# Another order of the input units and small copies by ScalarE instead of GpSimd, in a hybrid SSD, S5 and attention layer

## The chip, the core and the metric

The kernel runs on one core of a Trainium2 chip. The metric is the device time of one launch in microseconds (us). Each run of a kernel is timed several times and the median is given. A profile is one further execution, with its own time. The engines are PE (TensorE, matmuls), DVE (VectorE), ACT (ScalarE), POOL (GpSimd) and SP (SyncE, which issues nearly all DMAs here).

## The reference, cut to what matters

One layer of a streaming encoder on 528 prompt positions (16 of them learned) and 64 sample positions, 592 columns in all, D_MODEL = 1024. One input projection feeds three branches.

```python
h = rmsnorm(x, lp['norm_mix'])
y_a, conv_new, ssd_new = ssd_branch(h, z, xbc, dt, ...)      # conv of width 4, silu, chunked scan, gate silu(z)
y_b, s5_re, s5_im = s5_branch(h @ w_u, ...)                  # complex diagonal scan
o_c = stick_breaking(q, [k_hist, k], [v_hist, v])            # attention with q/k norm
mix = gates[0]*(y_a @ w_lift_a) + gates[1]*glu(gelu(y_b)) + gates[2]*(o_c @ w_lift_c)
x = x + mix @ w_out
x = x + square(relu(rmsnorm(x) @ w_up)) @ w_down

def causal_dwconv(x, hist, w, b):
    xp = concatenate([hist, x], axis=1)
    y = b + sum(xp[:, k:k + T] * w[k] for k in range(4))
    return y, xp[:, -3:]                                     # the last three columns are an output
# s5_branch:  x_t = a * x_{t-1} + B u_t (complex);  y = Re(C x) + d * u;  outputs also x at the last position
```

The convolution's last three input columns and the S5's last states, for prompt and sample, are outputs. All of it is float32.

## The kernel before, in words

**Units.** Every product with a weight is cut into units of 128 output columns (`units()`, L71). A unit's weights, 128 x 1024, are loaded by SP into one of three `w_raw` buffers (L287). ACT copies them rounded into `w_hi` (L253), DVE subtracts to get `w_lo` (L217, the line of the helper `tt`). PE then makes, for each half of the 592 columns, 24 matmuls: w_hi with the high and the low part of the activations (L336, L337), w_lo with the high part (L338). They go to one of three PSUM buffers (`ps_d`), which ACT, mostly, evacuates.

**The order of the units.** `ORDER` (L59) is a string that `mixed()` reads: x is a unit of the SSD's convolution input (`do_xbc`, ten), z one of its gate (`do_z`, eight), a, b, c the sums' gates. `units()` puts four u units (the S5's input) and twelve q, v, k units ahead of them, and the later products behind.

**An x unit.** `do_xbc` takes a tile `pre` (three buffers, tag "ea", shared with the q, k and v units), zeroes its first three columns (L559), copies three columns of the old state into it (L560), evacuates PSUM into it (L564 to L567), copies its edges into the output tile `conv_o` (L569, L570), and forms the convolution (`cv`: L572 on ACT, then L574 three times on DVE), its sigmoid and product (`cs`), which SP stores to `x_scr` (L578). `conv_out` (L1210) is stored once, when all ten are there.

**Beside the units.** The S5, the attention and the SSD are Python generators that are advanced a step at a time between units, by credits (`PACE`), so their instructions lie among the units' in each engine's order. The S5 (`s5()`) first has eight steps q, then a scan on DVE (L803), from which come `x_r` and `x_i` (DVE, tags d_r and d_i). Four copies, 128x16 each, put the last states into `so` (L816), which SP stores to `s5_out` (L817; the profile calls it s_out). `xs` is filled from x_r and x_i, half by ACT (L826) and half by DMA (L828). Eight iterations follow: in each, eight DMAs fill a tile `tz` (L834, two buffers, so that iteration 2's waits for PE's last use in iteration 0), and PE multiplies tz with `ub` (L847) and `oc` with `xs` (L849), in turns, into `ps_y`. ACT and DVE make y from it (`gsq`, L855 and L856; `y_sb`).

**Who sets the order.** A scheduler of the framework lists each engine's instructions once, ahead of time. Each engine then runs its own list strictly in order, waiting on semaphores where its inputs or buffers aren't ready. SP's list is one queue too: a DMA whose data isn't ready holds back all DMAs behind it.

Of the kernel before, what the change touches and what calls it, by code (L numbers as in the profile page):

```python
# [11 lines left out]
AF = mybir.ActivationFunctionType  # L12
# [4 lines left out]
TP, TS = 528, 64  # L17
# [8 lines left out]
XW = 3 + TP + 3 + TS  # L26
# [29 lines left out]
NC_ = _fields(CST, [("ident", 128), ("tri", 128), ("blk", 128), ("msk", 128), ("msk_s", 64), ("eye2", 16)])  # L56


ORDER = "x" * 10 + "z" * 8 + "a" * 8 + "b" * 8 + "c" * 8  # L59


def mixed():
    n = dict.fromkeys("xzabc", 0)
    out = []
    for c in ORDER:
        out.append(({"x": "xbc", "z": "z", "a": "g1", "b": "g2", "c": "g0"}[c], n[c]))
# [110 lines left out]
def body(tc, io):  # L177
    nc = tc.nc
    V, S, G, PE, SP = nc.vector, nc.scalar, nc.gpsimd, nc.tensor, nc.sync
# [4 lines left out]
    with ExitStack() as ctx:  # L184
# [13 lines left out]
        A = lambda n, i=0, w=1: pa[:, PA[n][0] + i:PA[n][0] + i + w]  # L198
# [17 lines left out]
        def tt(e, o, a, b, op):  # L216
            e.tensor_tensor(o, a, b, op=op)  # L217
# [31 lines left out]
        def sigmoid(a, out, scale=1.0):  # L249
            S.activation(out, a, AF.Sigmoid, scale=scale)  # L250
# [128 lines left out]
        def dense(u, xh, xl, evac, kt=8, base=0, w=None, parts=live, weave=False):  # L379
            if w is None:  # L380
                w, i = fetch(u)
                ahead(i)
            if weave:
                pss = [psd.tile([128, 512], F32, name="ps_d", tag="d") for _ in parts]
                for k in range(kt):
                    for ps, cols in zip(pss, parts):
                        mm3(ps[:, :cols.stop - cols.start], w[0], w[1], 1, xh[:, k:k + 1], xl[:, k:k + 1], cols,
                            base=base + k, start=k == 0, stop=k == kt - 1)
                for ps, cols in zip(pss, parts):
                    evac(cols, ps[:, :cols.stop - cols.start])  # L390
                return w
            for cols in parts:
                n = cols.stop - cols.start
                ps = psd.tile([128, 512], F32, name="ps_d", tag="d")
                mm3(ps[:, :n], w[0], w[1], kt, xh, xl, cols, base=base)
                with urgent():
                    evac(cols, ps[:, :n])
                side(kt)
            return w
# [32 lines left out]
        for k in range(8):  # L432
            x, g = xt[:, k, :], gm[:, k:k + 1]
# [59 lines left out]
        conv_o = keep.tile([128, 10, 6], F32, name="conv_o", tag="conv_o")  # L493
# [10 lines left out]
        def etile(n, tag, w=T, dt=F32):  # L504
            return ev.tile([128, 608], dt, name=n, tag=tag, bufs=BUFS[tag])[:, :w]
# [51 lines left out]
        def do_xbc(m):  # L557
            pre = etile("pre", "ea", XW)
            G.memset(pre[:, 0:3], 0.0)  # L559
            G.tensor_copy(pre[:, 3 + TP:6 + TP], A("state_conv", 3 * m, 3))  # L560

            def evac(cols, ps):
                if cols.start == 0:
                    S.activation(pre[:, 3:3 + H], ps, AF.Copy)  # L564
                else:
                    S.activation(pre[:, 3 + H:3 + TP], ps[:, :TP - H], AF.Copy)
                    S.activation(pre[:, 6 + TP:], ps[:, TP - H:], AF.Copy)  # L567
            dense(("xbc", m), hh, hl, evac, parts=halves)
            G.tensor_copy(conv_o[:, m, 0:3], pre[:, TP:TP + 3])  # L569
            G.tensor_copy(conv_o[:, m, 3:6], pre[:, XW - 3:XW])  # L570
            c = etile("cv", "eb", CW)
            S.activation(c, pre[:, 0:CW], AF.Identity, scale=A("conv_w", 4 * m), bias=A("conv_b", m))  # L572
            for k in range(1, 4):
                V.scalar_tensor_tensor(c, pre[:, k:k + CW], A("conv_w", 4 * m + k), c, op0=OP.mult, op1=OP.add)  # L574
            s = etile("cs", "ec", CW)
            sigmoid(c, s)
            tt(V, s, s, c, OP.mult)
            SP.dma_start(x_scr[m], s)  # L578
# [141 lines left out]
        def s5():  # L720
# [30 lines left out]
            for q in range(8):  # L751
# [18 lines left out]
                z = psg.tile([128, 512], F32, name="ps_bs", tag="g")  # L770
# [11 lines left out]
                m = [sp.tile([128, 2, NX], F32, name="mo%d" % j, tag="mo%d" % j) for j in range(4)]  # L782
# [30 lines left out]
            tt(V, fl(x_i), fl(x_i), yy[:, 0, :], OP.add)  # L813
            so = new("so", [128, 4, 16])
            for j, (xx, c) in enumerate(((x_r, NB), (x_i, NB), (x_r, NX - 1), (x_i, NX - 1))):
                G.tensor_copy(so[:, j, :], xx[:, :, c])  # L816
            SP.dma_start(io["s5_out"], so)  # L817
            yield

# [9 lines left out]
            for it in range(8):  # L829
# [29 lines left out]
                if it % 2:  # L859
                    m = it // 2  # L860
# [562 lines left out]
        n1.release()  # L1423
        do_dt()
        pulls.append((s5(), PACE["s5"]))
        for m in range(4):
            do_qk("q", m, qg, q_scr, live)
# [3 lines left out]
        for n, m in mixed():  # L1431
            if n == "xbc":
                do_xbc(m)
                if m == 9:
                    pulls.append((ssd(), PACE["ssd"]))
            elif n == "z":
                do_z(m)
            else:
                do_gate(int(n[1]), m)
# [32 lines left out]
        for m2 in range(4):  # L1472
            w = None
            for j in range(2):
                m = 2 * m2 + j
# [25 lines left out]
        for m in range(8):  # L1501
            x = etile("xr", "eb")
# [159 lines left out]
```

## Time and profile before

| | |
|---|---|
| median of 3 runs | 1120.91 us (1119.19 to 1122.09) |
| the profiled execution | 1120.97 us, span 1119.2 us |
| mean granted clock | 0.994 |
| PE busy | 1100.5 us, 98% |
| DVE, ACT, POOL busy | 794.3, 539.6, 183.7 us |

The profile gives the busy time of each engine, windows (busy time, count of instructions and the granted TensorE clock of a stretch; 1.00 is 2.4 GHz), the chain of waits that ended last, and timelines. In a window's row the columns are the engines PE, PEld (weight load), DVE, ACT and POOL. A wait is written behind an arrow with the instruction that ended it. The S5's end (scan, states, eight iterations) lies between 193 and 281 us in this trace.

### The profile page before, as it was taken

Reading aid. Unit: us, or ns where it says so; the run is one execution under the profiler, and the core shown is the slowest. Engines: PE = TensorE matmul, PEld = TensorE weight load, DVE = VectorE, ACT = ScalarE, POOL = GpSimd, SP = SyncE. Lnnn points to the kernel's source line nnn. Section 1 sums busy time; section 2 is a strip of 40 time slices with the busy share of each in tenths; the row PEclk is TensorE's granted clock in tenths of the full one; section 3 lists DMA queues with packets and bytes.
Section 4 is the critical chain, followed back from the end, with each engine's and each line's share of the span. In section 5 each row is a group of like instructions: output and inputs, shape, how many; then the busy total and the mean of one; then the engine's idle time right before and its main releaser. Section 6 shows DMA issues by size and latency. Waiting matters only on the chain.

```text
span 1119.2 us, 21309 instructions
## 1 busy us (share of the span) xinstructions
PE 1100.5 (98%) x8532; PEld 1061.7 (95%) x8532; DVE 794.3 (71%) x1377; ACT 539.6 (48%) x896; POOL 183.7 (16%) x240
## 2 busy tenths in 40 slices
PE   9999999999999999999998999999999999999998
PEld 8998999999998999898788999999999999999998
DVE  7968579955667475549988754467866785786787
ACT  6455465523365455465668323355444444444443
POOL 2086256611000000005422300300000000000000
PEclk9999999989999999999999999999999999999999
DMA  7663224466754353277445543322232223223222
GB/s 275 147 145 115 84 90 125 110 165 165 241 177 138 113 179 133 89 255 257 129 146 167 151 134 99 99 75 94 76 102 88 75 77 115 74 76 129 79 81 80
DMA packets 80594, 144.04 MB, mean 129 GB/s; under 512 B 26512, under 2 KB 40688, under 8 KB 79984
## 3 DMA queue, kind: packets, MB, share of 16 engines
q1 hardware_dynamic: 80496, 142.69, 41.0%
q8 instruction: 67, 1.10, 0.4%
q14 instruction: 31, 0.25, 0.1%
HBM read 117.40 MB, written 24.38 MB: 127 GB/s over the span
## 4 chain that ended last, share of the span: by engine, by line
PE 80%; DVE 10%; POOL 3%; ACT 2%; DMA 2%; issue 2%; SPq 1%; DVEq 0%; ACTq 0%; POOLq 0%
PE ps_d L336 18%; PE ps_d L337 18%; PE ps_d L338 18%; PE ps_x L1581 3%; PE ps_x L1580 3%; PE ps_x L1582 3%; PE ps_o L895 2%; PE ps_z L895 2%; PE ps_y L1581 1%; PE ps_y L1580 1%; PE ps_y L1582 1%; DVE w_lo L217 1%; DVE ar L1272 1%; DVE ar L217 1%; POOL cm L217 1%
## 5 line engine op out<-in xcount | busy, mean ns | idle before, releaser
L336 PE MATMUL ps_d<-hh,w_hi 128*128 128x288 f32 (+1 forms) x864 | 260.5, 301 | 0.0
L338 PE MATMUL ps_d<-hh,w_lo 128*128 128x288 f32 (+1 forms) x864 | 260.0, 301 | 0.0
L337 PE MATMUL ps_d<-hl,w_hi 128*128 128x288 f32 (+1 forms) x864 | 260.0, 301 | 0.0
L253 ACT ACTIVATE w_hi<-w_raw 128x1024 fp32r<-128x1024 f32 (+1 forms) x150 | 151.8, 1012 | 220.7 <-PE ps_d L337 142.8
L217 DVE TENSOR_TENSOR w_lo<-w_raw,w_hi 128x1024 fp32r<-128x1024 f32 (+1 forms) x150 | 179.2, 1195 | 104.2 <-ACT w_hi L253 103.7
L337 PEld LDWEIGHTS ps_d<-hl,w_hi 128*128 128x128 f32 x864 | 164.5, 190 | 0.9 <-issue 0.3
L338 PEld LDWEIGHTS ps_d<-hh,w_lo 128*128 128x128 f32 x864 | 164.7, 191 | 0.5
L336 PEld LDWEIGHTS ps_d<-hh,w_hi 128*128 128x128 f32 x864 | 164.7, 191 | 0.4
L336 PE MATMUL ps_d<-x2h,w_hi 128*128 128x288 f32 x512 | 151.3, 296 | 0.0
L337 PE MATMUL ps_d<-x2l,w_hi 128*128 128x288 f32 x512 | 151.1, 295 | 0.0
L338 PE MATMUL ps_d<-x2h,w_lo 128*128 128x288 f32 x512 | 150.3, 295 | 0.0
L338 PEld LDWEIGHTS ps_d<-x2h,w_lo 128*128 128x128 f32 x512 | 96.2, 188 | 0.1
L336 PEld LDWEIGHTS ps_d<-x2h,w_hi 128*128 128x128 f32 x512 | 96.2, 188 | 0.1
L337 PEld LDWEIGHTS ps_d<-x2l,w_hi 128*128 128x128 f32 x512 | 96.2, 188 | 0.0
L253 ACT ACTIVATE w_hi<-ws 128x1024 fp32r<-128x1024 f32 x32 | 34.0, 1061 | 55.0 <-PE ps_y L1581 21.7
L1581 PE MATMUL ps_x<-ftl,w_hi 128*128 128x288 f32 x192 | 56.7, 295 | 0.5 <-DVE ftl L217 0.5
L1580 PE MATMUL ps_x<-fth,w_hi 128*128 128x288 f32 x192 | 56.8, 296 | 0.2 <-ACT s L1600 0.2
L1582 PE MATMUL ps_x<-fth,w_lo 128*128 128x288 f32 x192 | 56.4, 294 | 0.0
L1531 ACT ACTIVATE fr<-ps_d 128x288 f32<-128x288 f32 x64 | 25.7, 402 | 55.8 <-PE ps_d L338 55.8
L217 POOL TENSOR_TENSOR xe<-xd,tend 128x1024 f32<-128x1024 f32 (+2 forms) x6 | 11.6, 1942 | 234.4 <-DVE xd L217 210.1
L217 DVE TENSOR_TENSOR w_lo<-ws,w_hi 128x1024 fp32r<-128x1024 f32 x32 | 39.0, 1220 | 12.6 <-ACT w_hi L253 12.6
L906 DVE TENSOR_TENSOR_SCAN aw<-col,aw 128x400 f32<-128x400 f32 (+4 forms) x36 | 30.7, 899 | 17.3 <-ACT aw L250 17.2
(472 smaller groups left out, 2727.1 us busy)
## 6 DMA issues: line engine op xcount, KB each, us to landing
w_raw<-wts SPq DMA_DIRECT2D x150, 512.0 KB, 3.5
g_scr<-go SPq DMA_DIRECT2D x24, 288.0 KB, 2.8
gt<-g_scr SPq DMA_DIRECT2D x24, 288.0 KB, 3.1
ar<-ac_scr SPq DMA_DIRECT2D x4, 1024.0 KB, 7.2
x_scr<-cs SPq DMA_DIRECT2D x10, 297.5 KB, 2.9
xc<-x_scr SPq DMA_DIRECT2D x4, 640.0 KB, 7.0
xt<-xT SPq DMA_DIRECT2D x8, 296.0 KB, 5.7
z_scr<-zs SPq DMA_DIRECT2D x8, 288.0 KB, 4.6
```

The costliest lines, as they stand in the source:

```text
L217: e.tensor_tensor(o, a, b, op=op)
L253: S.activation(hi, x, AF.Copy)
L336: PE.matmul(ps, wh[:, c], xh[:, k, cols], start=start and k == 0, stop=False)
L337: PE.matmul(ps, wh[:, c], xl[:, k, cols], start=False, stop=False)
L338: PE.matmul(ps, wl[:, c], xh[:, k, cols], start=False, stop=stop and k == kt - 1)
L895: mm = lambda *a, **b: PE.matmul(*a, skip_group_check=True, **b)
L906: V.tensor_tensor_scan(x, one.to_broadcast([128, n]), x, 1.0, op0=OP.mult, op1=OP.mult)
L1272: V.tensor_scalar(ar[:n, h, :n], ar[:n, h, :n], acm[:n, c, h:h + 1], 0.0, op0=OP.subtract, op1=OP.min)
L1531: S.activation(r[:, cols], ps, AF.Relu)
L1580: PE.matmul(ps, w[0][:, o], fh[:, k], start=first and k == 0, stop=False, skip_group_check=True)
L1581: PE.matmul(ps, w[0][:, o], fl[:, k], start=False, stop=False, skip_group_check=True)
L1582: PE.matmul(ps, w[1][:, o], fh[:, k], start=False, stop=k == 3, skip_group_check=True)
```

## The change

The string of units begins with four z units, then the ten x units, then the other four z units. Three lines of `do_xbc` and one of `s5()` copy with ScalarE (`S.activation`, function Copy) what GpSimd copied: ten times three copies of 128x3, and four of 128x16.

```diff
-ORDER = "x" * 10 + "z" * 8 + "a" * 8 + "b" * 8 + "c" * 8
+ORDER = 'zzzzxxxxxxxxxxzzzzaaaaaaaabbbbbbbbcccccccc'
@@ do_xbc
-            G.tensor_copy(pre[:, 3 + TP:6 + TP], A("state_conv", 3 * m, 3))
+            S.activation(pre[:, 3 + TP:6 + TP], A("state_conv", 3 * m, 3), AF.Copy)
@@ do_xbc, behind dense(("xbc", m), ...)
-            G.tensor_copy(conv_o[:, m, 0:3], pre[:, TP:TP + 3])
-            G.tensor_copy(conv_o[:, m, 3:6], pre[:, XW - 3:XW])
+            S.activation(conv_o[:, m, 0:3], pre[:, TP:TP + 3], AF.Copy)
+            S.activation(conv_o[:, m, 3:6], pre[:, XW - 3:XW], AF.Copy)
@@ s5
-                G.tensor_copy(so[:, j, :], xx[:, :, c])
+                S.activation(so[:, j, :], xx[:, :, c], AF.Copy)
```

The numbers behind names are those of buffers; they differ between the two kernels. First SP's queue of the kernel before, from the second half of `xs` to the `tz` loads of the S5's third iteration (cs_2858 belongs to the eighth x unit):

```order
L828 DMA xs1_2385<-x_r_2323 64x1216
L828 DMA xs0_2384<-x_i_2324 64x1216
L817 DMA s5_out<-so_2331 128x64
L287 DMA w_raw_3164<-wts 128x1024
L578 DMA x_scr_223<-cs_2858 128x595
L1210 DMA conv_out<-conv_o_234 128x60
L834 DMA tz_2627<-kd_scr_225 16x4x128 x8
```

The same place in the kernel after (cs_2705 belongs to the second x unit):

```order
L828 DMA xs1_2362<-x_r_2311 64x1216
L828 DMA xs0_2361<-x_i_2312 64x1216
L817 DMA s5_out<-so_2319 128x64
L287 DMA w_raw_3021<-wts 128x1024
L578 DMA x_scr_223<-cs_2705 128x595
L834 DMA tz_2583<-kd_scr_225 16x4x128 x8
```

The x units stand later against the S5 there, so the store of `conv_out`, which needs all ten, has gone behind.

Next GpSimd's list of the kernel before, round the copies into `so`, with the edges of the last three x units (pre_2862, pre_2963, pre_3058):

```order
L569 COPY conv_o_234<-pre_2862 128x3
L570 COPY conv_o_234<-pre_2862 128x3
L816 COPY so_2331<-x_r_2323 128x16
L569 COPY conv_o_234<-pre_2963 128x3
L570 COPY conv_o_234<-pre_2963 128x3
L816 COPY so_2331<-x_i_2324 128x16
L816 COPY so_2331<-x_r_2323 128x16
L816 COPY so_2331<-x_i_2324 128x16
L559 MEMSET pre_3058 128x3
L560 COPY pre_3058<-pa_81 128x3
L569 COPY conv_o_234<-pre_3058 128x3
L570 COPY conv_o_234<-pre_3058 128x3
```

In the kernel after, ScalarE's list has these copies, here round `so`:

```order
L569 ACTIVATE conv_o_234<-pre_2818 128x3
L570 ACTIVATE conv_o_234<-pre_2818 128x3
L572 ACTIVATE cv_2910<-pre_2818,pa_81 128x595
L816 ACTIVATE so_2319<-x_r_2311 128x16
L826 ACTIVATE xs0_2361<-x_r_2311 64x1216
L816 ACTIVATE so_2319<-x_i_2312 128x16
L816 ACTIVATE so_2319<-x_r_2311 128x16
L816 ACTIVATE so_2319<-x_i_2312 128x16
L826 ACTIVATE xs1_2362<-x_i_2312 64x1216
L250 ACTIVATE cs_2705<-cv_2700 128x595
```

The copies stand between ScalarE's own work on x_r and x_i, behind the third x unit's L572. GpSimd keeps only the memsets L559 of this stretch.

Last, ScalarE's list of the kernel after where the state of the third x unit is copied into its `pre` (pre_2709), among the z units that now come first (`zs` is a z unit's evacuation, `rr` belongs to the S5's steps q):

```order
L253 ACTIVATE w_hi_2419<-w_raw_2221 128x1024
L250 ACTIVATE zs_2326<-ps_d_2381 128x288
L768 ACTIVATE rr_2108<-ps_r_2099 128x512
L560 ACTIVATE pre_2709<-pa_81 128x3
L250 ACTIVATE zs_2418<-ps_d_2425 128x288
L253 ACTIVATE w_hi_2511<-w_raw_2331 128x1024
L250 ACTIVATE zs_2418<-ps_d_2471 128x288
L564 ACTIVATE pre_2508<-ps_d_2517 128x296
```

The copy into pre_2709, which needs a buffer of tag "ea" to be free, stands ahead of evacuations of a z unit and of a weight's `w_hi`; in the kernel before it stood on GpSimd's list.

## Rows read from the trace of the kernel before

**Rows 1.** The page: busy time, share of the span and instructions of each engine.

```profile
PE 1100.5 (98%) x8532; PEld 1061.7 (95%) x8532; DVE 794.3 (71%) x1377; ACT 539.6 (48%) x896; POOL 183.7 (16%) x240
```

**Rows 2.** Windows of 40 us: length, PE, PEld, DVE, ACT, POOL, clock, DMA, GB/s.

```profile
200.00:240.00 40.00, 37.58 (x252) 37.38 (x251) 31.50 (x40) 17.60 (x30) 21.11 (x16) 0.87 0.55 150
...
840.00:880.00 40.00, 40.00 (x303) 40.00 (x302) 27.85 (x42) 17.52 (x32) 0.00 (x0) 1.00 0.25 82
```

**Rows 3.** The waits of PE: us in total, times, longest us.

```profile
PE ps_y L847 <- DMA tz<-kd_scr: 2.4, 1, 2.4
```

**Rows 4.** Timeline of PE: start us, us, what, idle before and its releaser.

```profile
218.07 0.39 PE L847 MATMUL ps_y<-ub,tz 128*128 128x73 f32 x2
...
228.44 0.67 PE L847 MATMUL ps_y<-ub,tz 128*128 128x73 f32 x2 [2.42 <-DMA tz<-kd_scr]
...
594.20 0.40 PE L336 MATMUL ps_d<-ybx,w_hi 128*128 128x288 f32 x1 [1.75 <-DVE mix L217]
```

**Rows 5.** Windows round the waits and the low clock.

```profile
228.40:238.90 10.50, 10.46 (x46) 10.49 (x47) 4.29 (x9) 1.98 (x5) 2.86 (x2) 0.51 0.71 198
238.90:249.40 10.50, 10.50 (x84) 10.50 (x83) 5.42 (x9) 3.89 (x7) 1.11 (x1) 1.00 0.43 89
282.00:287.00 5.00, 5.00 (x28) 4.95 (x28) 3.85 (x18) 1.80 (x3) 0.00 (x0) 0.66 0.82 248
...
596.00:606.00 10.00, 10.00 (x74) 9.83 (x74) 8.73 (x22) 7.69 (x12) 1.43 (x1) 1.00 0.75 258
```

**Rows 6.** Timeline of SP's DMA issues, 213 to 227 us.

```profile
213.11 0.46 SPq L828 DMA_DIRECT2D xs<-x_i  x1
220.62 0.35 SPq L817 DMA_DIRECT2D s_out<-so  x1
...
222.49 4.45 SPq L834 DMA_DIRECT2D tz<-kd_scr  x8
```

**Rows 7.** The chain that ended last, at the wait: start us, us, what.

```profile
226.51 1.80 DMA tz<-kd_scr
```

**Rows 8.** Timeline of POOL, 213 to 221 us.

```profile
213.07 1.96 POOL L816 COPY so<-x_r 128x16 f32<-128x16 f32 x1
...
217.14 0.82 POOL L816 COPY so<-x_i 128x16 f32<-128x16 f32 x1
217.91 1.94 POOL L816 COPY so<-x_r 128x16 f32<-128x16 f32 x1
219.79 0.81 POOL L816 COPY so<-x_i 128x16 f32<-128x16 f32 x1
...
220.59 0.18 POOL L560 COPY pre<-pa 128x3 f32<-128x3 f32 x1
```

**Rows 9.** Timeline of DVE, 211 to 217 us.

```profile
211.66 1.42 DVE L217 TENSOR_TENSOR x_i<-x_i,yy 128x1216 f32<-128x1216 f32 x1
...
213.75 1.22 DVE L217 TENSOR_TENSOR w_lo<-w_raw,w_hi 128x1024 fp32r<-128x1024 f32 x1
214.88 1.58 DVE L574 SCALAR_TENSOR_TENSOR cv<-pre,pa,cv 128x595 f32<-128x595 f32 x2
216.38 0.77 DVE L217 TENSOR_TENSOR cs<-cs,cv 128x595 f32<-128x595 f32 x1
```

**Rows 10.** ACT by line and form, 140 to 300 us: busy, mean ns, idle before.

```profile
L567 ACT ACTIVATE pre<-ps_d 128x64 f32<-128x64 f32 x10 | 2.2, 217 | 0.0
...
L826 ACT ACTIVATE xs<-x_r 64x1216 f32<-64x1216 f32 x1 | 1.2, 1222 | 0.6 <-DVE x_r L217 0.6
```

**Rows 11.** The DMAs into tile tz, all 64 of them.

```profile
DMA to landing us min/median/max: 1.7/1.9/6.2
```

**Rows 12.** Timeline of ACT, 220 to 223 us.

```profile
220.80 0.88 ACT L572 ACTIVATE cv<-pre,pa 128x595 f32<-128x595 f32 x1 [3.63 <-POOL pre L560]
...
222.18 0.39 ACT L855 ACTIVATE gsq<-ps_y 128x292 f32<-128x292 f32 x1
```

**Rows 13.** DMA issues, 140 to 300 us: count, KB each, us to landing.

```profile
k_out<-qs SPq DMA_DIRECT2D x1, 296.0 KB, 2.1
```

## The prediction, made before the changed kernel was run

> **What bounds the kernel now.** I read the page's engine table first: PE is busy for 1100.5 of the span's 1119.2 us, DVE for 794.3, ACT for 539.6, POOL for 183.7 [rows 1]. Both kernels issue the same matmuls, so only two things can change the time: PE's idle time, and stretches in which its matmuls run longer. The table of 40-us windows shows where the second is. From 200 to 240 us PE issued 252 rows of matmuls at a granted clock of 0.87 and was busy for 37.58 us; from 840 to 880 it issued 303 at 1.00 [rows 2]. This is the only long stretch below full clock, and it lies where the S5 branch ends and the ten x units run.
>
> The list of PE's waits has one entry above the others: one wait of 2.4 us of L847 (the S5's first product) for the DMA that fills tz [rows 3]. PE's timeline gives its place, 228.44 us, idle 2.42 before [rows 4]. The windows cut at this place show the price: from 228.4 to 238.9 us the granted clock is 0.51, the lower of the two levels (1.2 GHz), in the next 10.5 us it is 1.00 (2.4 GHz). The first window issues 46 matmul rows, the next 84 [rows 5]. An idle 1.75 us near 594 us had no such consequence: the window behind it (596 to 606 us) has clock 1.00 [rows 4, 5].
>
> Why is tz late? Its eight DMAs stand on SP's queue, which issues in order. SP's rows: second xs load at 213.11, then nothing for 7 us, s_out at 220.62, behind it three more loads and stores, and from 222.49 the tz loads, 4.45 us of issue [rows 6]. The last landed 1.80 us after its issue, which released PE [rows 7]. The buffer had been free since PE's last L847 of this buffer at 218.07 [rows 4], so the tz loads went out some 4 us later than the buffer allowed. What SP waited for is POOL: s_out stores the tile so, whose last copy ends at 220.60. The four copies by POOL (128x16) took 1.96, 0.82, 1.94 and 0.81 us, with two copies of the convolution's edges between them [rows 8]; conv_out, also ahead of tz, waits for the last of those.
>
> **The change part by part.** (1) *The order.* The same 34 units in other places: no matmul, DMA byte or DVE operation added. The S5's end (scan, x_r, x_i, so, tz of the third iteration) met x units before and meets x units after. By the two orders, PE has 54 matmuls of units between the last use of the buffer and the third iteration's first, 55 before; so PE wants tz at about the same distance from x_i as before. x_i ends at 211.66 + 1.42 = 213.08 [rows 9], and PE came to the wait at 228.44 - 2.42 = 226.02, so 12.9 us behind x_i. I count from the end of x_i in both.
>
> (2) *The four so copies on ScalarE.* The trace of before has no ACT row of 128x16. The nearest is L567, a copy of 128x64 in 217 ns; the longest form of a copy there, 64x1216, takes 1222 [rows 10]. I take 0.22. The copy of x_r can go before x_i is done; the other three end 0.66 us after x_i, and s_out goes out at +1.0 instead of 220.62 - 213.08 = +7.5. Upper bound: were ACT as slow as POOL's rows, 0.82 + 1.94 + 0.81 = 3.6 us, s_out goes out at +4.0.
> By the Trainium skill, "SBUF — State Buffer", section "Who interferes with whom", a GpSimd operation that reads SBUF and a VectorE operation with two SBUF inputs exclude each other for a whole instruction, while ScalarE has ports of its own. The trace agrees as to POOL: 1.96 us beside a busy DVE, and 0.18 for L560 (128x3) at 220.59, when DVE waited for ScalarE [rows 8]. By it the upper bound falls away; the sum is the same with either.
>
> (3) *The rest of SP's queue before tz.* Behind s_out stand a weight load, one x_scr and then tz; conv_out has gone behind. The weight load needs a buffer that DVE's w_lo frees. By the order, two cv and one w_lo follow x_i; the rows start 216.38 - 214.88 = 1.50 us apart for two cv and 214.88 - 213.75 = 1.13 for a w_lo [rows 9], so +2.6. The x_scr needs cs: two more cv and cs, 1.50 + 0.77, so +4.9, issued by +5.3. PE frees the tz buffer at 218.07 + 0.4 = +5.4 as before. So tz goes from +5.6, against 222.49 - 213.08 = +9.4. From the first issue to the last landing it took 226.51 + 1.80 - 222.49 = 5.8 us, so all has landed at +11.4, 1.5 us before PE asks at +12.9. Each landing takes 1.7 us at least, 1.9 in the middle, 6.2 at most [rows 11]; a walk with somewhat slower landings of xs gives a margin of 1.0. The stall of 2.42 us goes, and with it the clock's fall.
>
> (4) *What the fall cost.* Two estimates from [rows 5]: 46 matmuls at the next window's 84 in 10.5 us would take 5.75, so 4.75 us lost; by the clock, 10.5 x (1 - 0.51) = 5.15. I take 5.0.
>
> (5) *The 30 copies of the convolution's edges and the 4 of so as load on ACT.* 34 x 0.22 = 7.5 us on an engine busy 539.6 of 1119.2 us. In the 40 us from 200, with x units and the S5's end, ACT was busy 17.60 [rows 2]; an x unit is 48 matmuls of 10.5 / 84 = 0.125 us, some 6 us [rows 5], so three copies add 0.66 to about 2.7 in each and are hidden by PE's matmuls. If that cover is gone, the bound is 7.5 us. POOL's removal from this place takes a wait away too: ACT's cv at 220.80 had been idle for 3.63 us behind POOL's L560 [rows 12]. No gain on PE follows, since that wait did not end at PE. From below: nothing.
>
> (6) *What is late next.* tz for the fourth to eighth iteration. PE has 72, 52, 71, 54 and 73 matmuls of units between a buffer's last use and the next first use by the new order, and had 74, 45, 72, 46 and 74. By the same walk the margins are 1.8, 1.2, over 1, 1.2 and -0.3 us; the last is what before shows as well (a landing 0.3 us after PE came), at no visible fall. The fall of 282 to 287 us (clock 0.66, 5 x 0.34 = 1.7 us lost [rows 5]) follows the small matmuls of the S5's last two iterations and of a dt product (L1148); these are adjacent in the new order too, so I keep it: bounds 0 and -1.7.
>
> Sum: -2.42 - 5.0 = -7.4. The profiled execution took 1120.97 us (span 1119.2), as good as the median 1120.91. Forecast 1113.5 us.
>
> **The rivals.** *A, the wait stays or moves.* The margin of 1.0 to 1.5 us is eaten when one of the eight loads lands as slowly as the slowest did, 6.2 us: then tz comes at +11.4 + 4.3 = +15.7 and PE stands 2.8 us, as before, and the clock falls. [...] It gives 1120.97 - 7.4 + 7.4 to 8.0, 1119 to 1122. Waits up to 1.75 us would cost only themselves (as near 594 us): 1114 to 1115.3; that lies in the forecast's own range.
>
> *B, slower: ACT's queue blocked.* POOL could wait for a buffer at no cost; ACT evacuates PSUM and makes w_hi. Two of the new L560 copies stand in ACT's order ahead of evacuations of z units and wait for a pre buffer, which is free only when an earlier q or k store has landed. PE fills three PSUM buffers, each from 24 matmuls of 0.125 us = 3.0 us, before it stands: from a block of about 5 us longer than the store needs, PE stalls over 2 us. Two such stalls with a fall cost 2 x 7.4, so 1120.97 - 7.4 + 14.8 = 1128.4. For it: ACT was held 3.63 us behind POOL's L560 once in before [rows 12]. Against: by the order these stores are issued a unit or more earlier, and a k_out store landed in 2.1 us [rows 13].
> The Trainium skill, "TensorE: Matmul & The Clock Gate", section "Architectural detail: the array is 16× 32×32, not 1× 128×128", says that ScalarE's queue is strictly first in, first out; the trace agrees: behind the wait of 3.63 us the next instructions went in order, gsq at 222.18 [rows 12], though the matmuls that it reads had begun by 218.07 [rows 4]. It is the rule by which this change could lose.
>
> *C, better.* The fall at 282 goes too, since other work now stands before it: 1113.5 - 1.7 = 1111.8.
>
> **How the numbers follow.** Forecast 0.66, with its own range 1111.5 (clock bound 5.15, small waits of half a microsecond gone) to 1116.5 (a wait of 1.75 us and 1.2 of exposed ACT work). A 0.18, B 0.08, C 0.08. The range holds forecast and C and the larger part of A: 1111.3 to 1121.3. What a measurement of this kernel can tell from no change is 0.3%, 3.4 us: faster is below 1117.5, slower above 1124.3. Faster 0.66 + 0.08 = 0.74, same 0.18, slower 0.08.
>
> **What would show it.** In the profile after: no wait of L847 for tz above 1 us; no 10-us window below clock 0.9 in the x units; s_out issued within 1.5 us behind x_i and the third iteration's tz within 6; so copies on ACT of 0.2 to 0.3 us each. Wrong would be: a PE wait above 2 us at any L847 or L849, a clock of 0.5 for 10 us elsewhere, an evacuation L564 or w_hi late behind an L560.

## The result and the profile after

The changed kernel takes 1128.01 us (1124.21 to 1130.12, 6 runs), the kernel before 1120.04 us (1117.03 to 1122.09, 6 runs): a ratio of 1.0064, with a 95% interval of 1.0048 to 1.0080. It is slower by 0.6%, where 1113.5 us and a gain of 0.7% were forecast.

The profiled execution took 1130.12 us, 9.2 us more than that of before. Its engine table [rows 1 for before]:

```profile
PE 1103.1 (98%) x8532; PEld 1063.5 (94%) x8532; DVE 795.1 (70%) x1377; ACT 543.8 (48%) x930; POOL 152.5 (14%) x206
```

The list of PE's waits in the kernel after, against the one long wait of [rows 3] (us in total, times, longest):

```profile
PE ps_d L336 <- DVE zs L217: 3.3, 1, 3.3
PE ps_x L1252 <- DVE cb L217: 2.3, 1, 2.3
PE ps_y L847 <- DMA tz<-kd_scr: 2.3, 2, 2.0
...
PE ps_y L849 <- DMA xs<-x_i: 1.4, 1, 1.4
```

Windows of 20 us of the kernel after show where the clock fell:

```profile
140.00:160.00 20.00, 16.33 (x124) 15.64 (x123) 12.16 (x25) 9.06 (x18) 6.19 (x12) 0.89 0.24 83
160.00:180.00 20.00, 20.00 (x166) 19.24 (x165) 10.66 (x25) 10.09 (x15) 4.05 (x8) 0.94 0.32 97
220.00:240.00 20.00, 20.00 (x154) 20.00 (x153) 19.49 (x26) 10.37 (x26) 3.97 (x5) 1.00 0.64 157
280.00:300.00 20.00, 18.02 (x117) 17.63 (x116) 9.35 (x39) 4.51 (x8) 0.83 (x4) 0.83 0.65 175
500.00:520.00 20.00, 17.71 (x116) 15.63 (x116) 12.67 (x24) 12.68 (x15) 9.42 (x4) 0.91 0.52 172
600.00:620.00 20.00, 18.25 (x123) 17.81 (x122) 16.90 (x36) 15.62 (x24) 3.77 (x2) 0.91 0.58 179
```

The stretch in which the kernel before lost most (220 to 240 us, [rows 2, 5]) is whole: clock 1.00, no idle PE. The forecast gain is there. But four other stretches have idle time and a low clock; of these only the one from 280 us was below full clock before (0.91 in the same window, by the fall of [rows 5]). The first and costliest, read as the chain of waits of the kernel after (start us, us, what; pieces of 0.01 to 0.04 us named "issue" between these lines are left out):

```profile
152.86 0.38 PE ps_q L539
153.24 0.15 PE ps_q L540
153.41 0.52 ACT rsl L243
153.95 0.45 ACT rq L244
154.42 1.28 ACT L250
155.71 0.42 ACT zs L250
156.16 0.47 DVE zs L217
156.67 0.61 PE ps_d L336
```

The instruction of 1.28 us without a tile name is ScalarE's load of a function table for the sigmoid (ACT_TABLE_LOAD in the timeline below). PE has just made `ps_q`, the key norm's sum of squares (the last k unit, whose norm runs on beside the first z unit). ScalarE's list holds the norm's Ln (L243) and Exp (L244), then the table load, and only then `zs`, the sigmoid that evacuates the first z unit's PSUM, and DVE multiplies after it. By then PE had filled all three PSUM buffers: its next matmul starts at 156.67, after 3.30 us idle. ScalarE's timeline of the kernel after shows that it had waited itself (idle before and its releaser in brackets):

```profile
150.21 0.21 ACT L560 ACTIVATE pre<-pa 128x3 f32<-128x3 f32 x1 [0.97 <-DMA q_scr<-qs]
153.41 0.51 ACT L243 ACTIVATE rsl<-ps_q,col 128x296 f32<-128x296 f32 x1 [2.99 <-PE ps_q L540]
...
154.42 1.28 ACT L250 ACT_TABLE_LOAD   x1
```

So ScalarE waited 2.99 us for `ps_q`, which stands on PE's list behind the z unit's matmuls, and the z unit's evacuation waited behind ScalarE. In the kernel before the same Ln (at 157.42) stands behind the evacuations of two x units (L564 to L567, here their first halves), which need neither that table nor DVE; ScalarE's timeline of before:

```profile
144.09 0.42 ACT L564 ACTIVATE pre<-ps_d 128x296 f32<-128x296 f32 x1
...
152.97 0.42 ACT L564 ACTIVATE pre<-ps_d 128x296 f32<-128x296 f32 x1 [2.15 <-PE ps_d L338]
...
157.42 0.51 ACT L243 ACTIVATE rsl<-ps_q,col 128x296 f32<-128x296 f32 x1
```

The clock then falls as it did at 228 us before. Windows of the kernel after:

```profile
156.00:160.00 4.00, 3.33 (x14) 3.33 (x15) 2.04 (x5) 1.17 (x4) 0.00 (x0) 0.50 0.19 74
160.00:164.00 4.00, 4.00 (x26) 3.98 (x26) 0.09 (x1) 1.10 (x2) 0.00 (x0) 0.70 0.00 2
```

The account, from waits and from (1 - clock) x 20 us of the windows. Gone: the stall and fall at 228 us, 2.42 + 0.26 x 20 = 7.6. New: at 153 us 3.30 and 0.37 idle + (0.11 + 0.06) x 20 = 7.1; for xs 1.4; for tz near 281 us 2.0 and a fall deeper by 1.6 (0.83 against 0.91); near 508 us 2.3 + 1.8; near 602 us 1.8. Together 18.0 - 7.6 = 10.4 against 9.2 measured. By the engine tables PE's idle time (span less busy time) grew by 6.5 us and its busy time by 2.6; the account has 7.0 of idle time and 3.4 of low clock, so its estimates of the clock are the rougher part.

### The profile page after: what moved, and what is told of

The parts are those of the page before. It is cut to its first block, busy times and chain, and to the rows that moved or that the text cites. A ratio compares the mean times of both kernels' runs of the same rounds, so it can differ in the third digit from the quotient of the medians.

```text
span 1128.3 us, 21293 instructions
## 1 busy us (share of the span) xinstructions
PE 1103.1 (98%) x8532; PEld 1063.5 (94%) x8532; DVE 795.1 (70%) x1377; ACT 543.8 (48%) x930; POOL 152.5 (14%) x206
## 4 chain that ended last, share of the span: by engine, by line
PE 78%; DVE 9%; ACT 4%; DMA 4%; issue 2%; POOL 2%; SPq 1%; DVEq 0%; ACTq 0%; POOLq 0%
PE ps_d L336 18%; PE ps_d L337 18%; PE ps_d L338 18%; PE ps_x L1581 3%; PE ps_x L1580 3%; PE ps_x L1582 3%; PE ps_o L895 2%; PE ps_z L895 2%; PE ps_y L1581 1%; PE ps_y L1580 1%; PE ps_y L1582 1%; DVE ar L1272 1%; DVE w_lo L217 1%; DMA ar<-ac_scr 1%; DMA w_raw<-wts 1%
```

## The experiments

**The changed kernel again (after_again).** No edit.

> The changed kernel once more, to see which of its waits recur. Theory A (the order of units is to blame: the first z unit's sigmoid stands on ScalarE's list behind the key norm's Ln, Exp and a table load, so PE runs out of PSUM buffers at 153 us): the wait of PE for zs near 153 us recurs at 3.3 us, and a low clock behind it, since it follows from the lists. The wait of 2.0 us for tz near 281 us recurs too. The wait of 2.3 us near 508 us hangs on one slow DMA (9.9 us) and may be absent; the low clock at 600 us, behind a wait of 1.75 us that the kernel before has as well, may be absent too. Then the time is 1123 to 1128. Theory B (the copies put on ScalarE's list are to blame, since one of them waited 0.97 us for the q store at 149 us and held what stood behind): the same waits recur; this run does not tell A from B.

It took 1128.46 us (1124.34 to 1130.03, 6 runs; ratio 1.0074, 1.0052 to 1.0095), half a microsecond above the upper end of what was expected. Here and below, ratios are to the kernel before as it was timed beside that run. The profiled execution is the fastest of them, 1124.34. The wait for zs recurs at 3.3 us, for xs at 1.4 and for tz at 1.7 us. The falls at 500 and 600 us do not:

```profile
500.00:520.00 20.00, 19.35 (x160) 17.23 (x160) 14.56 (x25) 9.69 (x14) 10.42 (x4) 1.00 0.56 185
600.00:620.00 20.00, 18.71 (x138) 18.27 (x138) 18.72 (x37) 15.10 (x21) 7.49 (x4) 1.00 0.61 199
```

So 4 to 6 us of the changed kernel's 1130 belong to single executions, not to its lists; the stall at 153 us belongs to the lists.

**The order of units alone (order_only).** The kernel before with the new string only.

```diff
-ORDER = "x" * 10 + "z" * 8 + "a" * 8 + "b" * 8 + "c" * 8
+ORDER = 'zzzzxxxxxxxxxxzzzzaaaaaaaabbbbbbbbcccccccc'
```

> The new order of units alone; all 34 copies stay on GpSimd. Theory A: the wait for zs at 153 us stays (3.0 to 3.5 us, clock 0.5 behind it), and tz of the third S5 iteration may be late again, since GpSimd's copies of so are slow beside VectorE: 1124 to 1134 us. Theory B: the wait for zs at 153 us is gone or below 1 us: 1117 to 1123 us.

1124.36 us (1124.27 to 1129.36, 6 runs; ratio 1.0054, 1.0034 to 1.0073). Its waits of PE:

```profile
PE ps_y L847 <- issue: 3.6, 1, 3.6
PE ps_d L336 <- DVE zs L217: 3.3, 1, 3.3
```

The profiled execution is the slowest of the six, 1129.36 us, 5 us above the median, so not every wait in it is typical. The wait for zs is there at full size without one copy on ScalarE. Theory B falls: the copy into `pre` that waited 0.97 us for the q store was hidden by the wait for `ps_q`, which ended later. The 3.6 us lie at 283.70 us, at the S5's last iteration; the view names no releaser.

The new order alone also took away most of the stall at 228 us: tz of the third iteration came 1.1 us late, and the clock stayed whole. PE's timeline of this kernel, then a window:

```profile
228.42 0.41 PE L847 MATMUL ps_y<-ub,tz 128*128 128x73 f32 x2 [1.11 <-DMA tz<-kd_scr]
```

```profile
220.00:240.00 20.00, 18.89 (x144) 18.68 (x144) 19.49 (x26) 8.70 (x17) 11.63 (x14) 1.00 0.52 143
```

So the 5 us of the median are a balance: the stall at 153 us and what is late at the S5's end, less most of the old stall.

**The copies alone (copies_only).** The changed kernel with the old string.

```diff
-ORDER = 'zzzzxxxxxxxxxxzzzzaaaaaaaabbbbbbbbcccccccc'
+ORDER = "x" * 10 + "z" * 8 + "a" * 8 + "b" * 8 + "c" * 8
```

> The 34 copies on ScalarE alone, with the order of before (ten x units, then eight z units). Theory A: no wait of PE at 140 to 165 us; s_out goes out within 1.5 us behind x_i, tz of the third iteration is in time, no low clock at 228 us: 1112 to 1116 us, and this version beats both. Theory B: a wait of PE of 2 us or more at 140 to 180 us behind a copy into pre that waits for a store: 1122 to 1130 us.

1114.53 us (1113.51 to 1115.88, 6 runs; ratio 0.9958, 0.9942 to 0.9974): faster than both, by some 5 and 14 us. The mean clock of the profiled execution is 1.000. SP's timeline of this kernel shows the queue as the prediction worked it out, s_out 0.6 us behind the end of x_i (213.40) and tz from 219.43, 6.0 us behind it [rows 6 for before]:

```profile
213.43 0.46 SPq L828 DMA_DIRECT2D xs<-x_i  x1
213.99 0.83 SPq L817 DMA_DIRECT2D s_out<-so  x1
...
219.43 4.69 SPq L834 DMA_DIRECT2D tz<-kd_scr  x8
```

and ScalarE's timeline the copies at the length that was taken:

```profile
213.44 0.23 ACT L816 ACTIVATE so<-x_i 128x16 f32<-128x16 f32 x1
213.58 0.21 ACT L816 ACTIVATE so<-x_r 128x16 f32<-128x16 f32 x1
```

The window of the old stall and that of the old fall at 282 us are whole:

```profile
220.00:240.00 20.00, 20.00 (x158) 20.00 (x157) 15.87 (x27) 7.39 (x15) 2.68 (x2) 1.00 0.58 157
280.00:300.00 20.00, 20.00 (x153) 20.00 (x152) 14.25 (x51) 6.62 (x14) 1.56 (x2) 1.00 0.87 242
```

**Two x units ahead of the four z units (x2z4).**

```diff
-ORDER = 'zzzzxxxxxxxxxxzzzzaaaaaaaabbbbbbbbcccccccc'
+ORDER = 'xxzzzzxxxxxxxxzzzz' + 'a' * 8 + 'b' * 8 + 'c' * 8
```

> The changed kernel with two x units ahead of the four z units (x x z z z z, eight x, four z). On ScalarE's list the evacuations of these x units stand ahead of the key norm's last steps and the table load. Theory A: the wait for zs at 153 us is gone (below 1 us), with the low clock behind it, which is 7 us off the changed kernel: 1117 to 1122 us. Theory B: the copies into pre stand where they stood, so a wait of 2 us or more stays at 150 to 165 us, and the time stays at 1124 to 1130 us.

1136.58 us (1130.42 to 1139.97, 6 runs; ratio 1.0142, 1.0116 to 1.0168). The wait at 153 us is gone, as theory A has it (and B does not); a wait of 0.97 us for another zs remains at 170 us. But the time is a miss for both theories: new waits stand far behind the edit, in the stage of the GLU and the first sums. PE's timeline of this kernel:

```profile
527.50 0.61 PE L336 MATMUL ps_d<-ybx,w_hi 128*128 128x288 f32 x1 [3.87 <-ACT go L250]
...
569.94 0.61 PE L336 MATMUL ps_d<-ybx,w_hi 128*128 128x288 f32 x1 [5.55 <-DVE mix L217]
```

**The first two z units evacuated by a plain copy (z_copy).** The changed kernel with one edit in `do_z`:

```diff
             s = etile("zs", "ec")
+            raw = etile("zr", "eb") if m < 2 else None

             def evac(cols, ps):
+                if m < 2:
+                    S.activation(raw[:, cols], ps, AF.Copy)
+                    ps = raw[:, cols]
                 sigmoid(ps, s[:, cols])
```

> The changed kernel, with one edit: the first two z units evacuate PSUM by a plain ScalarE copy into SBUF, and take sigmoid and product from there; on ScalarE's list these copies now stand ahead of the key norm's L243 and of the table load (some 1.6 us more ScalarE work). Theory A (PE ran out of PSUM buffers at 153 us because the first z unit's sigmoid, with its table load, stood behind the key norm on ScalarE's list): the wait for zs of 3.3 us and the low clock behind it go, 7 us in all; the waits for xs (1.4) and tz (1.7 to 2.0) stay: 1117 to 1122 us. Theory B (the copy into pre, which waits for a store and stays ahead of an evacuation in this list too, is to blame): a wait of 2 us or more stays, 1124 us or more.

1117.63 us (1115.06 to 1122.19, 12 runs; ratio to before 0.9989, 0.9975 to 1.0002), 8 to 10 us below the changed kernel (8 by the ratios to before, 10 by the medians). ScalarE's timeline shows the three evacuations ahead of the Ln, though a copy into `pre` still waits between them:

```profile
144.57 0.41 ACT L586 ACTIVATE zr<-ps_d 128x288 f32<-128x288 f32 x1
...
149.90 0.40 ACT L586 ACTIVATE zr<-ps_d 128x288 f32<-128x288 f32 x1
150.97 0.21 ACT L560 ACTIVATE pre<-pa 128x3 f32<-128x3 f32 x1 [0.67 <-DMA q_scr<-qs]
153.29 0.41 ACT L586 ACTIVATE zr<-ps_d 128x288 f32<-128x288 f32 x1 [2.11 <-PE ps_d L338]
...
157.31 0.49 ACT L243 ACTIVATE rsl<-ps_q,col 128x296 f32<-128x296 f32 x1
```

and the windows of the same kernel that PE is whole there and near 282 us, where the wait for tz has gone too:

```profile
140.00:160.00 20.00, 20.00 (x168) 19.75 (x167) 12.11 (x24) 10.80 (x22) 6.49 (x12) 1.00 0.20 71
...
280.00:300.00 20.00, 20.00 (x153) 20.00 (x152) 12.73 (x53) 3.95 (x7) 0.65 (x2) 1.00 0.66 179
```

Theory A stands: the stall is the place of the z unit's evacuation on ScalarE's list. What the table load has in it by itself (1.28 us of the chain) was not tried apart from the Ln and Exp ahead of it. More than 7 us came back. The later wait for tz went with it; but the changed kernel's median also holds the falls near 508 and 602 us, and z_copy has waits of 1.5 us at 214 us and 1.6 us at 307 us of its own, so how the rest divides is not shown.

**Four buffers for tz (tz4, z_copy_tz4, copies_tz4).** One edit, in the changed kernel, in z_copy and in the copies alone:

```diff
-                tz = sp.tile([128, 4, 128], F32, name="tz", tag="tz%d" % (it % 2))
+                tz = sp.tile([128, 4, 128], F32, name="tz", tag=("tz0", "tz1", "rr0", "rr1")[it % 4])
```

> The changed kernel with four buffers for tz in place of two (two of them lie where the S5's rr lay), so SP may issue an iteration's loads two iterations earlier. Theory A2 (the wait for tz near 282 us comes from SP's queue, where the loads of the last iterations stand behind x_scr, conv_out and z loads and start only when PE has freed a buffer): that wait and the low clock behind it shrink to below 0.5 us, 2 to 4 us off; the wait for zs at 153 us stays at 3.3 us: 1122 to 1127 us. Rival: the loads are late for the DMA traffic itself, then nothing changes: 1127 to 1129 us.

> Both edits in the changed kernel. If the waits at 153 and 282 us are all that its order of units costs, it comes to within 2 us of the copies alone in the old order (1114.5): 1113 to 1117 us. If the order costs something else besides (the wait for xs of 1.4 us is known), it stays at 1118 us or above.

> The 34 copies on ScalarE in the order of before, with four buffers for tz. The copies alone still have waits for tz of 0.76 and 1.03 us, at full clock; with four buffers they go: 1112 to 1114 us. Rival: the earlier loads collide with xs and x_scr and delay xs, then 1114 to 1117 us.

All three are far off on the slow side: 1136.80 us (1131.55 to 1139.83, 6 runs; ratio 1.0149, 1.0124 to 1.0174), 1132.41 (1131.51 to 1133.86, 4 runs; 1.0121, 1.0102 to 1.0140) and 1138.38 (1138.01 to 1140.32, 4 runs; 1.0176, 1.0157 to 1.0195). The waits for tz did go: none above 0.6 us is left in any of the three. Most of the time is lost in the stage where x2z4 lost it; PE's timeline of tz4:

```profile
525.79 0.61 PE L336 MATMUL ps_d<-ybx,w_hi 128*128 128x288 f32 x1 [3.90 <-ACT go L250]
...
567.10 0.61 PE L336 MATMUL ps_d<-ybx,w_hi 128*128 128x288 f32 x1 [5.55 <-DVE mix L217]
```

The lists say why these four kernels are alike. Read from the end backwards, ScalarE's list agrees with that of the copies alone in 671 instructions for the kernel before, 518 for the changed one, order_only and z_copy, but only 319 for x2z4 and the three with four buffers; VectorE's in 1020, 835 and 516. Those 319 reach back to the end of the GLU's products only, so the lists of these four differ from the others in that stage or ahead of it. The scheduler had written other lists for the middle of the kernel, far behind the edit. Why it does is not settled. So these runs do not tell what four buffers, or both edits together, would be worth, and the cause of the late tz at the S5's last iteration stays untested.

**The so copies alone (so_only) and the edges alone (edges_only).** The kernel before, with the line of `s5()` changed, or the three lines of `do_xbc`.

> The order of before; only the four copies into so go to ScalarE, the 30 copies of the convolution's edges stay on GpSimd. Theory C (s_out was late because the so copies stood on GpSimd beside a busy VectorE; conv_out behind it waits for the last edge copy, which GpSimd had done at 221 us only because of the so copies ahead of it): s_out goes within 1.5 us behind x_i, tz of the third iteration no longer waits 2.4 us, no low clock at 228 us: 1113 to 1117 us, as the copies alone. Rival: conv_out, still ahead of tz on SP's queue, waits for edge copies on GpSimd that are themselves slow (up to 4 us each), and tz stays late by 1 us or more: 1117 to 1121 us.

> The order of before; only the 30 copies of the edges go to ScalarE, the four into so stay on GpSimd. Theory C: the four so copies still take 0.8 to 2 us each, but start without edge copies between them, so s_out goes out some 5.5 to 6 us behind x_i in place of 7.5, tz lands about 1.5 to 2 us earlier, and the wait shrinks from 2.4 us to below 1: without the fall of the clock, 1114 to 1118 us. Rival: the wait stays at 2 us and the clock falls, 1118 to 1122 us.

1115.30 us (1113.49 to 1119.20, 12 runs; ratio 0.9963, 0.9947 to 0.9979) and 1114.81 (1113.16 to 1116.04, 7 runs; 0.9959, 0.9943 to 0.9974): either half removes the stall at 228 us, and neither can be told from both together. (The profiled execution of so_only is its slowest, 1119.20, with a wait for tz of 2.1 us at a later iteration.) In so_only s_out left 0.6 us behind x_i, but conv_out, ahead of tz, held it until 220.04 us, 7.2 us behind x_i, as its rival has; that was still in time for PE. In edges_only GpSimd's four so copies follow each other directly, 1.34, 0.76, 1.94 and 0.80 us, s_out leaves 3.5 us behind x_i's end at 214.59 (5.5 to 6 were expected), and SP issues tz from 220.33, 5.7 us behind it. SP's timeline of that kernel:

```profile
218.07 0.35 SPq L817 DMA_DIRECT2D s_out<-so  x1
...
220.33 5.05 SPq L834 DMA_DIRECT2D tz<-kd_scr  x8
```

So it was the two kinds of copy on one GpSimd list that made tz late, not the length of the so copies alone.

## Why the prediction was wrong, point by point

- *What bounds the kernel, and parts (2) to (4), the stall at 228 us and its price: right.* Copies alone gave 1120.97 - 1114.79 = 6.2 us between the profiled executions and 5 us between the medians, against 7.4. The stall and its fall went whole there, and the old fall at 282 us too, which was rival C; against that, two waits for tz of 0.76 and 1.03 us and one for xs of 0.6 us came up in that kernel. In the changed kernel itself s_out left 0.6 us behind x_i (1.0 worked out), tz from 5.3 us (5.6), so copies took 0.22 to 0.23 us (0.22; the upper bound by GpSimd's rows was far off), and PE began the third iteration at 227.10, 12.5 us behind x_i (12.9), without a wait for its tz. DVE's, SP's and PE's timelines of the kernel after:

```profile
213.23 1.42 DVE L217 TENSOR_TENSOR x_i<-x_i,yy 128x1216 f32<-128x1216 f32 x1
215.22 0.54 SPq L817 DMA_DIRECT2D s_out<-so  x1
219.90 3.69 SPq L834 DMA_DIRECT2D tz<-kd_scr  x8
227.10 0.34 PE L847 MATMUL ps_y<-ub,tz 128*128 128x73 f32 x2
```

By the Trainium skill, "SBUF — State Buffer", section "Who interferes with whom", ScalarE has SBUF ports of its own, which VectorE does not share. The trace agrees: the so copies by ScalarE took 0.22 to 0.23 us beside a VectorE that was busy with x_i and the convolution.

- *Part (1), the order of units at no cost: the step that failed.* "The same 34 units in other places: no matmul, DMA byte or DVE operation added." That is true and was not enough. I followed the move only at the S5's end, where x units meet the scan as before, and not at the front of the string, where z units now meet the last k unit. There an evacuation that needs a table load and a VectorE product took the place of one that is a plain copy, and stood behind the key norm's Ln. Its price was 7.1 us at that place. Order_only has the same stall without one copy moved: 3.3 us of wait for zs, and the windows from 140 and 160 us at 0.87 and 0.96. Its 5 us over the kernel before are less than that, since the order by itself also took away most of the stall at 228 us.
- *The wait for xs: in no term of the sum.* The "about the same distance" was worked out for tz, and there it held. The first use of xs got no term: in the kernel before PE began it at 217.01, 3.9 us behind the end of x_i; in the changed one PE was ready 2.0 us behind it (218.12 - 1.45 - 214.65) and waited 1.4 us in both executions, without a fall.
- *Part (6), margin of -0.3 us at the last iteration: too small.* The waits were 2.0, 1.7 and, in order_only, 3.6 us. With the first stall removed (z_copy) none above 0.6 us was left, so this wait seems to hang on what comes before; through what is not shown.
- *Rival B had the right engine and almost the right time (1128.4), by the wrong instruction.* ScalarE's queue did hold back the evacuation of z units, and the fall of the clock followed. But what held it were L243, L244 and the table load, which no edit added, not the copies into `pre`: their waits for a store lasted 0.97 us and did not reach PE, and with all of them on GpSimd the stall was the same 3.3 us. Its time was argued with two stalls; there was one, with three smaller things behind it. That it came so near is luck.
- *Rule of the queue.* What "TensorE: Matmul & The Clock Gate" of the Trainium skill says in "Architectural detail: the array is 16× 32×32, not 1× 128×128", that ScalarE's queue is strictly first in, first out, agrees with the chain above: zs, whose PSUM was full, ran only after Ln, Exp and the table load.
- *"Waits up to 1.75 us would cost only themselves": not always.* This was read from one wait of the kernel before; the last section has the same wait with a fall behind it.

Still open: why the clock fell near 508 and 602 us in one execution of the changed kernel and not in another, and why the scheduler writes other lists behind small edits.

## What to carry to other kernels

A unit that is moved meets new neighbours at both ends of its move: look on every engine's list at what stands ahead of its evacuation, above all an instruction that waits for the same engine that the evacuation is to set free. Try the parts of a change apart: here one part was worth -5 us and the other +5, and together they cost 8. The two do not add up, since each of them takes away most or all of the same stall at 228 us, and together they can do so only once. Where a scheduler writes the lists, compare the lists of the whole kernel after each edit: four of these versions lost 8 to 24 us, most of it in a stage that the edit didn't touch.

## What was not expected of the hardware

The same wait of 1.74 to 1.75 us near 600 us left the clock at 1.00 in the kernel before [rows 4, 5], in after_again and in the copies alone, and was followed by a fall (0.91 in the 20-us window) in the first execution of the changed kernel and in order_only. So one length of a wait can come with or without the fall. The same holds for a longer one: in copies_tz4 PE stood 3.02 us before a unit's first matmul, nearly the 3.30 us that were followed by a clock of 0.50 in the changed kernel, and the window stays whole. PE's timeline of copies_tz4, then the window:

```profile
231.81 0.40 PE L336 MATMUL ps_d<-hh,w_hi 128*128 128x288 f32 x1 [3.02 <-DVE zs L217]
```

```profile
220.00:240.00 20.00, 16.98 (x132) 16.83 (x132) 13.38 (x21) 7.51 (x13) 1.11 (x1) 1.00 0.80 246
```

The window behind it, 240 to 260 us, is at 1.00 too.

GpSimd's copies of 128x16 took from 0.20 to 2.09 us over these runs, ScalarE's of the same shape 0.21 to 0.23.
